# A low half of weights on GpSimd beside the convolution taps, and a seventh up tile by seven block products

## The chip, the cores and the metric

The kernel runs on one core of a Trainium2 chip. The metric is the device time of one execution in microseconds, the median of the runs shown. The engines are called by their short names: PE (TensorE, matrix products, with PEld for its weight loads), DVE (VectorE), ACT (ScalarE), POOL (GpSimd) and SP (the engine that issues most of the weight loads).

## The reference

Two layers on a sequence of 512 rows with 1024 channels, everything in 32-bit floats. Each layer has a mixer, a gated feed-forward network (FFN) with a short causal convolution, and a per-layer embedding. The change lies in the FFN, which each layer runs once:

```python
def conv_ffn(xn, w_up, conv_w, conv_b, w_down):
    S = xn.shape[1]
    h = xn @ w_up                                    # 1024 -> 2 x 2816 channels
    hp = jnp.pad(h, ((0, 0), (CONV_WIDTH - 1, 0), (0, 0)))
    c = conv_b + sum(hp[:, t:t + S] * conv_w[t] for t in range(CONV_WIDTH))
    g, u = jnp.split(c, 2, axis=-1)
    return (jax.nn.silu(g) * u) @ w_down             # 2816 -> 1024

for i in range(DEPTH):                               # DEPTH = 2
    xn = rmsnorm(h, norm_mix[i])
    h = h + (mixer_a(...) if i < 1 else mixer_b(...))
    h = h + conv_ffn(rmsnorm(h, norm_ffn[i]), ...)
    h = h + per_layer_embed(h, p[i], ...)
return rmsnorm(h, norm_final)
```

## The kernel before

**Products in halves.** A weight is cut into a high half `wh`, which ACT rounds (L203), and a low half `wl` = weight minus `wh`, which DVE subtracts (L204). The activations are cut in the same way. A product is three matmuls, high by high, high by low and low by high (`mm3`, L234). The channels lie on the partitions and the 512 rows of the sequence are the columns of the moving matrix.

**The weights' way.** SP fetches the weights piece by piece into staging buffers that take turns under three names (`staged`: `wraw`, and the sums `wsum` below). The halves of at most 1024 columns are called units. There are four buffers each for `wh` and `wl` (`WBUFS`), and `pump` writes the cast and the subtraction of a unit up to four units ahead of the matmuls that use it. A unit's buffer comes free only when PE has done with the unit four before it.

**The up tiles.** Each layer's FFN has 22 tiles of 2 x 128 up channels, here numbered 0 to 21. A plain tile is 48 matmuls of 512 columns (two PSUM banks, `up`, 8 blocks of the input, three products each) and two units of 1024 columns. A woven tile (the numbers in `UPS`) is made by seven products of blocks in Strassen's manner (`woven_up`): 84 matmuls of 256 columns, on sums of the inputs that are made once, and on four units (1024, 1024, 1024 and 512 columns) that come from the raw weights and from sums of them (`weave`, three DVE steps L163 to L165 on 512 to 1024 columns). The seven products end in two PSUM tiles `ux` and `uy`; ACT copies (`head`, `side`, L805), and DVE puts them together in SBUF (`minus`, L812, L813).

**After a tile.** `gated` (L755) applies the convolution: for each of the two halves an ACT pass with scale and bias (L760) gives `c`, and two DVE taps (L762) add the rows shifted by one and by two. They read PSUM where the tile is plain and SBUF where it is woven. Then come Silu on ACT and a product on DVE (L769). A class `Pair` takes two finished tiles and makes the sums that the woven down projection needs (L518 to L535, L312).

**The blocks.** The 22 tiles go in three blocks, 0 to 7, 8 to 15 and 16 to 21. Before the down projection of the first and of the second block, the first tile of the next one is already multiplied (tile 8, tile 16), so that DVE can work on its result beside the projection. The two first down projections are woven (`dx`, `dy`, four column chunks, each added to what DRAM holds), the third is plain (`d`). So from the end of tile 5 the order before is: tile 6 plain, tiles 7 and 8 woven, down projection; in the second block tiles 8, 9, 10, 12, 14 are woven, 11, 13, 15 plain, tile 16 woven ahead of the projection; in the third 17, 18, 20, 21 woven and 19 plain.

**Order.** The code is written out by a scheduler that puts each instruction on its engine's queue in the order that its estimate of readiness gives. `behind(a, b)` holds `a` after `b` on the same engine without a semaphore. An engine does its queue in order: a step that waits holds all behind it.

Of the kernel before, what the change touches and what calls it, by code (L numbers as in the profile page):

```python
# [8 lines left out]
F32 = mybir.dt.float32  # L9
F32R = mybir.dt.float32r  # L10
AF = mybir.ActivationFunctionType
ALU = mybir.AluOpType

P = 128
D = 1024
S = 512
# [3 lines left out]
NJ = FF // P  # L20
PARTS = [(0, 8), (8, 16), (16, 22)]
WOVEN = 2
UPS = (7, 8, 9, 10, 12, 14, 16, 17, 18, 20, 21)
ASIDE = {7: 12, 9: 7, 17: 7, 20: 6}
PAIRS = 4
SLOTS = 9
# [26 lines left out]
def tile_yoco(ctx: ExitStack, tc: tile.TileContext, t, out: bass.AP, out_b: bass.AP):  # L53
    nc = tc.nc

    const = ctx.enter_context(tc.tile_pool(name="const", bufs=1))
# [5 lines left out]
    tp = ctx.enter_context(tc.tile_pool(name="tp", bufs=2))  # L62
# [4 lines left out]
    def psum(name):  # L67
        return mmp.tile([P, S], F32, tag="mm", name=name)
# [35 lines left out]
    def plan_ups(l, j0, j1):  # L104
        for j in range(j0, j1):
            (plan_woven if j in UPS else plan_cols)(t["w_up"][l, j : j + 1], 1, *((0, KD) if j in UPS else (KD,)))

# [29 lines left out]
                      [(ap, f"ah{q}", f"al{q}") for q in free[k0 : k0 + 4]] if c else None)  # L137

    units = [(i, q, lo, n) for i, p in enumerate(pieces) for q, (lo, n) in enumerate(p[2])]
    raws, ready, splits, sums = {}, {}, {}, {}  # L140
    state = {"raw": 0, "unit": 0, "next": 0, "tags": [0, 1, 2], "turn": 2, "pt": 0, "sent": {}}

    def behind(ins, front):

        tc.add_manual_dep(ins.ins, front.ins.name,
                          mybir.DependencyInfo(mybir.DependencyClass.NoSync, mybir.DependencyReason.DATA),
                          reason="order")

    def staged(name):
        tags = state["tags"]  # L150
        r = wp.tile([P, 2 * UNIT], F32, tag=f"r{tags[state['turn'] % len(tags)]}", bufs=1, name=name)
        state["turn"] += 1
        return r
# [25 lines left out]
    def pump(upto):  # L179
        while state["unit"] < min(upto, len(units)):  # L180
            i, q, lo, n = units[state["unit"]]
            load(i + 1)
            u = state["unit"]
            own = pieces[i][3]
            if own:
                pool, *tags = own[q]
                wh, wl = (pool.tile([P, n], F32R, tag=tg, name=f"own{u}_{tg}") for tg in tags)
            else:
                wh = wp.tile([P, UNIT], F32R, tag="wh", bufs=WBUFS, name=f"wh{u}")
                wl = wp.tile([P, UNIT], F32R, tag="wl", bufs=WBUFS, name=f"wl{u}")  # L190
            if i in woven:
                src = weave(i, q)
                hi, low = (x[:, :n].rearrange("p (b k m) -> p b k m", b=src.shape[1], m=P) for x in (wh, wl))
            elif i in paired:
                whole = raws[i][:, : pieces[i][1]].rearrange("p (c k n) -> p k c n", c=2, n=256)
                src = whole[:, lo // S : (lo + n) // S]
                hi, low = (x[:, :n].rearrange("p (k c n) -> p k c n", c=2, n=256) for x in (wh, wl))
            else:
                src, hi, low = raws[i][:, lo : lo + n], wh[:, :n], wl[:, :n]
            if u == 0:  # L200
                cast = nc.vector.tensor_copy(hi, src)
            else:
                cast = nc.scalar.copy(hi, src)  # L203
            state["split"] = splits[u] = cast, nc.vector.tensor_sub(low, src, hi.bitcast(F32))  # L204
            ready[u] = (wh, wl, n)
            state["unit"] += 1

    def take():
        u = state["next"]
        pump(u + 1)  # L210
        state["next"] += 1
        return ready.pop(u)
# [38 lines left out]
    def v(name, i):  # L251
        c = VEC[name] + i
        return vec[:, c : c + 1]
# [27 lines left out]
    ps = psum("idle").rearrange("p (a b) -> p a b", a=4)  # L281
    for i in range(IDLE):
        nc.tensor.matmul(ps, idle, idle.rearrange("p (o t) -> p o t", o=1).to_broadcast([P, 4, P]),
                         start=True, stop=True)
    minus_half = const.tile([P, S // 64], F32, name="minus_half")
    nc.vector.memset(minus_half, -0.5)
    ident = const.tile([P, P], F32, name="ident")
# [177 lines left out]
    box = {}  # L465
# [264 lines left out]
    def ffn(l, norm, nxt):  # L730
# [6 lines left out]
        def up(j, later=False):  # L737
            if j in UPS:
                return woven_up(j, later)
            parts = chunk(256, KD)  # L740
            pss = [psum(f"up{j}_{s}") for s in range(2)]
            if j:
                for s in range(2):
                    mm3(pss[s], parts, xs, s * P)
            else:
                for k, ((wh, wl, off), (xh, xl)) in enumerate(zip(parts, xs)):
                    for x, both in ((xh, (wh, wl)), (xl, (wh,))):
                        for s, ps in enumerate(pss):
                            for w in both:
                                nc.tensor.matmul(ps, w[:, off + s * P : off + (s + 1) * P], x,  # L750
                                                 start=k == 0 and x is xh and w is wh, stop=k == KD - 1 and x is xl)
            return pss if later else gated(j, pss)

        def gated(j, pss, fronts=()):
            cs = []  # L755
            for s, ps in enumerate(pss):
                col = s * NJ + j
                cw = [v("conv_w", (l * 3 + i) * 2 * NJ + col) for i in range(3)]
                c = tp.tile([P, S], F32, tag=f"c{s}", name=f"c{j}_{s}")
                nc.scalar.activation(c, ps, AF.Identity, bias=v("conv_b", l * 2 * NJ + col), scale=cw[2])  # L760
                for tap in (1, 2):
                    ins = nc.vector.scalar_tensor_tensor(c[:, tap:], ps[:, : S - tap], cw[2 - tap], c[:, tap:],  # L762
                                                         op0=ALU.mult, op1=ALU.add)
                    if fronts and tap == 1:
                        behind(ins, splits[fronts[s]][1])
                cs.append(c)
            a = tp.tile([P, S], F32, tag="sg", name=f"a{j}")
            box["silu"] = nc.scalar.activation(a, cs[0], AF.Silu)
            nc.vector.tensor_mul(a, a, cs[1])  # L769
            return a  # L770
# [51 lines left out]
        ins = inputs()  # L822
        ahead = up(0)
        behind(splits[state["next"] + 1][1], norm.low)
        for i, (j0, j1) in enumerate(PARTS):
            if i < WOVEN:
# [10 lines left out]
                pss, res = up(j1, later=True), []  # L837
                u = state["next"]
# [103 lines left out]
    for q, k0, k1 in FIRST:  # L942
# [4 lines left out]
        if k0 == 0:  # L947

            (wh, wl, off), = parts
            for x, w, cs in [(x, w, (c, c + 1)) for c in (0, 2) for x, w in ((0, wh), (0, wl), (1, wh))]:  # L950
                for c in cs:
                    nc.tensor.matmul(vps[q][c], xs[0][x][:, c * P : (c + 1) * P], w[:, off : off + S],
                                     start=x == 0 and w is wh, stop=False)
            continue
        if (q, k1) == (0, KD):
# [7 lines left out]
            cast, low = state["split"]  # L963
# [63 lines left out]
    for c in range(4):  # L1027
# [27 lines left out]
    ps = psum("turned")  # L1055
# [287 lines left out]
    last = len(steps)  # L1343
# [56 lines left out]
    pss = [psum(f"gt{i}_0") for i in range(2)]  # L1400
# [236 lines left out]
```

## Time and profile before

| | us |
|---|---|
| timed runs, median of 3 | 1100.64 (1100.06 to 1100.65) |
| span of the profiled execution | 1098.7 |
| median less span | 1.9 |
| PE busy | 1089.1 |
| DVE busy | 959.0 |
| ACT busy | 661.0 |
| GpSimd busy | 125.0 |

The granted TensorE clock is 0.999 over the span. A timeline's row reads: start (us from the span's start), duration, engine, line, operation, result<-operands, shape, count; what stands in square brackets is the idle time just before it and what ended it. A row of stretches has the length, then for each engine its busy time and the instructions that it began, then the granted clock, the DMA engines' share and GB/s. A row of waits has the engine, what waited, what it waited for, and the sum, count and longest of these waits.

### The profile page before, as it was taken

The numbers are of one execution on the slowest core, as the hardware profiler recorded it, in microseconds if no ns is written. First come the engines' busy times: TensorE is split into PE (matmuls) and PEld (weight loads), VectorE is DVE, ScalarE is ACT, GpSimd is POOL, SyncE is SP. The second block draws the span as 40 slices with busy tenths as digits, with TensorE's granted clock in tenths as the row PEclk, the third lists the DMA queues.
The fourth block names the chain that finished last, engine by engine and source line by source line (L and its number), as shares of the span: only waits on it lengthen the run. The fifth ranks groups of instructions, "written<-read, shape, count | busy, mean of one in ns | idle before, by whom it ended". The sixth has DMA issues, their size and how long they took to land.

```text
span 1098.7 us, 17476 instructions
## 1 busy us (share of the span) xinstructions
PE 1089.1 (99%) x6629; PEld 974.4 (89%) x6629; DVE 959.0 (87%) x1540; ACT 661.0 (60%) x1141; POOL 125.0 (11%) x192
## 2 busy tenths in 40 slices
PE   9999999999999999999999999999999999999997
PEld 7888988899998999988888887888999989999886
DVE  5588889999899989877988997799998999898887
ACT  5735666565676656655656775565655666567544
POOL 2200200000100010021114452000001000100200
PEclk9999999999999999999999999999999999999999
DMA  9621674125633267353234216441255333664534
GB/s 317 113 88 39 178 264 150 43 77 116 155 115 116 79 160 222 120 190 112 67 87 135 78 58 227 176 153 39 77 142 128 115 116 86 156 220 142 203 95 98
DMA packets 47508, 144.24 MB, mean 131 GB/s; under 512 B 13048, under 2 KB 18688, under 8 KB 36928
## 3 DMA queue, kind: packets, MB, share of 16 engines
q1 hardware_dynamic: 40560, 128.77, 35.6%
q0 software_dynamic: 5296, 9.70, 6.7%
q10 hardware_dynamic: 1568, 4.65, 1.1%
q8 instruction: 52, 0.85, 0.3%
q14 instruction: 32, 0.26, 0.1%
HBM read 116.89 MB, written 18.88 MB: 124 GB/s over the span
## 4 chain that ended last, share of the span: by engine, by line
PE 95%; DVE 2%; issue 1%; ACT 1%; DMA 0%; SPq 0%; POOLq 0%; POOL 0%; ACTq 0%
PE up L234 20%; PE ux L234 10%; PE dx L234 10%; PE uy L234 8%; PE dy L234 8%; PE d L234 6%; PE q L234 4%; PE gate L234 4%; PE u L234 4%; PE o L234 4%; PE up L750 2%; PE pv L1326 1%; PE v L244 1%; PE v L245 1%; PE v L246 1%; PE pin L234 1%
## 5 line engine op out<-in xcount | busy, mean ns | idle before, releaser
L204 DVE TENSOR_TENSOR wl<-wraw,wh 128x1024 fp32r<-128x1024 f32 (+2 forms) x198 | 217.3, 1102 | 42.8 <-ACT wh L203 41.9
L203 ACT CAST wh<-wraw 128x1024 fp32r<-128x1024 f32 (+2 forms) x197 | 182.8, 933 | 107.6 <-PE up L234 21.8
L203 ACT CAST wh<-wsum 128x1024 fp32r<-128x1024 f32 x84 | 88.3, 1052 | 62.7 <-issue 14.9
L204 DVE TENSOR_TENSOR wl<-wsum,wh 128x1024 fp32r<-128x1024 f32 x84 | 102.5, 1225 | 16.1 <-ACT wh L203 16.0
L762 DVE SCALAR_TENSOR_TENSOR c<-up,vec,c 128x511 f32<-128x511 f32 (+1 forms) x88 | 65.0, 744 | 2.4 <-ACT c L760 1.9
L234 PE MATMUL up<-nf10h,wh 128*128 128x512 f32 x160 | 62.3, 389 | 0.0
L234 PE MATMUL up<-nf00h,wh 128*128 128x512 f32 x160 | 62.3, 389 | 0.0
L234 PE MATMUL up<-nf10l,wh 128*128 128x512 f32 x160 | 62.3, 389 | 0.0
L234 PE MATMUL up<-nf00l,wh 128*128 128x512 f32 x160 | 62.3, 389 | 0.0
L234 PE MATMUL up<-nf00h,wl 128*128 128x512 f32 x160 | 62.1, 389 | 0.0
L234 PE MATMUL up<-nf10h,wl 128*128 128x512 f32 x160 | 62.0, 389 | 0.0
L600 POOL DMA_DIRECT2D saved<-head x16 | 13.9, 871 | 412.9 <-DVE head L720 412.9
L760 ACT ACTIVATE c<-up,vec 128x512 f32<-128x512 f32 x44 | 34.0, 777 | 31.8 <-PE up L234 26.6
L163 DVE TENSOR_TENSOR wsum<-wraw 128x1024 f32<-128x1024 f32 x42 | 51.2, 1220 | 0.6
L234 PE MATMUL ux<-t,wh 128*128 128x256 f32 x264 | 50.4, 283 | 0.0
L234 PEld LDWEIGHTS ux<-t,wh 128*128 128x128 f32 x264 | 41.2, 192 | 0.0
L234 PE MATMUL ux<-t,wl 128*128 128x256 f32 x132 | 37.4, 283 | 0.0
L234 PEld LDWEIGHTS up<-nf00h,wl 128*128 128x128 f32 x160 | 30.0, 188 | 6.2
L234 PEld LDWEIGHTS up<-nf10h,wl 128*128 128x128 f32 x160 | 30.0, 188 | 6.2
L234 PEld LDWEIGHTS up<-nf00l,wh 128*128 128x128 f32 x160 | 30.0, 188 | 6.2
L234 PEld LDWEIGHTS up<-nf10l,wh 128*128 128x128 f32 x160 | 30.0, 188 | 6.2
L234 PEld LDWEIGHTS up<-nf10h,wh 128*128 128x128 f32 x160 | 30.0, 188 | 6.0
(769 smaller groups left out, 3734.3 us busy)
## 6 DMA issues: line engine op xcount, KB each, us to landing
wraw<-in_w_up SPq DMA_DIRECT2D x44, 1024.0 KB, 5.6
wraw<-in_w_down SPq DMA_DIRECT2D x16, 1024.0 KB, 5.0
wraw<-in_w_gate SPq DMA_DIRECT2D x8, 1024.0 KB, 5.5
wraw<-in_w_down SPq DMA_DIRECT2D x8, 768.0 KB, 4.5
wraw<-in_w_u SPq DMA_DIRECT2D x4, 1024.0 KB, 9.4
wraw<-in_w_out SPq DMA_DIRECT2D x4, 1024.0 KB, 4.9
saved<-head POOLq DMA_DIRECT2D x16, 256.0 KB, 4.2
saved<-tail POOLq DMA_DIRECT2D x16, 256.0 KB, 4.1
```

The lines of the kernel that those rows point to most:

```text
L163: nc.vector.tensor_add(s[:, 0::3], g[:, 1:2].to_broadcast([P, 2, k, P]), g[:, 0::3])
L203: cast = nc.scalar.copy(hi, src)
L204: state["split"] = splits[u] = cast, nc.vector.tensor_sub(low, src, hi.bitcast(F32))
L234: return [nc.tensor.matmul(ps, w, x, start=first and j == 0, stop=last and j == len(todo) - 1, skip_group_check=onto) for j, (w, x) in enu ...
L244: nc.tensor.matmul(ps, xh[:, s], wh[:, a:b], start=st, stop=False)
L245: nc.tensor.matmul(ps, xl[:, s], wh[:, a:b], start=False, stop=False)
L246: nc.tensor.matmul(ps, xh[:, s], wl[:, a:b], start=False, stop=en)
L600: box["onto"] = nc.gpsimd.dma_start(x, y, accum_op=ALU.add)
L750: nc.tensor.matmul(ps, w[:, off + s * P : off + (s + 1) * P], x, start=k == 0 and x is xh and w is wh, stop=k == KD - 1 and x is xl)
L760: nc.scalar.activation(c, ps, AF.Identity, bias=v("conv_b", l * 2 * NJ + col), scale=cw[2])
L762: ins = nc.vector.scalar_tensor_tensor(c[:, tap:], ps[:, : S - tap], cw[2 - tap], c[:, tap:], op0=ALU.mult, op1=ALU.add)
L1326: nc.tensor.matmul(ps, lhs, rhs, start=j == 0, stop=j == len(todo) - 1)
```

## The change

Three things change.

- Tile 6 becomes woven (`UPS` gains 6). So tiles 6, 7 and 8 are woven in a row, ahead of the first down projection, in each layer.
- In each tile that stays plain (0 to 5, 11, 13, 15, 19) the order of the gating changes: both ACT passes come first, then a DVE copy of one column of the second one's result, called `sign`, then the four taps in the order first half, second half, first, second. All four are held behind the copy.
- One unit that stands two ahead of the next one to be taken at that moment gets its low half from GpSimd instead of DVE, and GpSimd starts it when the copy `sign` is done (`after`, with a semaphore). There are 20 such units.

The instructions of PE grow by 72 matmuls (2 x 36), those of DVE and ACT by 14 each, those of GpSimd by 20.

```diff
-UPS = (7, 8, 9, 10, 12, 14, 16, 17, 18, 20, 21)
+UPS = (6, 7, 8, 9, 10, 12, 14, 16, 17, 18, 20, 21)
...
+    def after(ins, front):
+
+        tc.add_manual_dep(ins.ins, front.ins.name,
+                          mybir.DependencyInfo(mybir.DependencyClass.Sync, mybir.DependencyReason.DATA),
+                          reason="start")
...
-            state["split"] = splits[u] = cast, nc.vector.tensor_sub(low, src, hi.bitcast(F32))
+            start = shadows.pop(u, None)
+            lows = (nc.gpsimd if start else nc.vector).tensor_sub(low, src, hi.bitcast(F32))
+            if start:
+                after(lows, start)
+            state["split"] = splits[u] = cast, lows
...
+    sign = const.tile([P, 1], F32, name="sign")
...
-            return pss if later else gated(j, pss)
+            return pss if later else gated(j, pss, shadow=True)
...
+            if shadow:
+                taps = []
+                for s, ps in enumerate(pss):
+                    col = s * NJ + j
+                    c = tp.tile([P, S], F32, tag=f"c{s}", name=f"c{j}_{s}")
+                    nc.scalar.activation(c, ps, AF.Identity, bias=v("conv_b", l * 2 * NJ + col),
+                                         scale=v("conv_w", (l * 3 + 2) * 2 * NJ + col))
+                    taps += [(c, ps, tap, v("conv_w", (l * 3 + 2 - tap) * 2 * NJ + col)) for tap in (1, 2)]
+                    cs.append(c)
+                with tc.high_priority():
+                    last = nc.vector.tensor_copy(sign, cs[1][:, :1])
+                    shadows[state["next"] + 2] = last
+                    for c, ps, tap, w in taps[::2] + taps[1::2]:
+                        ins = nc.vector.scalar_tensor_tensor(c[:, tap:], ps[:, : S - tap], w, c[:, tap:],
+                                                             op0=ALU.mult, op1=ALU.add)
+                        behind(ins, last)
+                        last = ins
+                a = tp.tile([P, S], F32, tag="sg", name=f"a{j}")
+                box["silu"] = nc.scalar.activation(a, cs[0], AF.Silu)
+                nc.vector.tensor_mul(a, a, cs[1])
+                return a
```

**Where it moves instructions.** The first place is DVE's row at the end of tile 5 in layer 0, before. `c5_0` and `c5_1` are tile 5's two halves, `wl51` is the first low half of tile 7 (tile 6 is still plain here, and its two units are older), `a5` is the gated tile, and `t03` an input sum.

```order
L762 SCALAR_TENSOR_TENSOR c5_0_2199<-up5_0_2149,vec_84,c5_0_2199 128x510
L204 TENSOR_TENSOR wl51_2228<-wraw26_2225,wh51_2227 128x1024
L312 TENSOR_TENSOR t03_2134<-x0_1sq_2126,t02_2133 128x512
L204 TENSOR_TENSOR wl52_2236<-wsum26_2229,wh52_2235 128x1024
L762 SCALAR_TENSOR_TENSOR c5_1_2203<-up5_1_2150,vec_84,c5_1_2203 128x511
L762 SCALAR_TENSOR_TENSOR c5_1_2203<-up5_1_2150,vec_84,c5_1_2203 128x510
L769 TENSOR_TENSOR a5_2207<-a5_2207,c5_1_2203 128x512
```

After, at the same place (`wl52` is the last unit of tile 6, `wl53` the first of tile 7; GpSimd's one here is `wl51`, tile 6's third unit):

```order
L323 TENSOR_TENSOR t03_2140<-x0_1sq_2132,t02_2139 128x512
L777 COPY sign_132<-c5_1_2211 128x1
L780 SCALAR_TENSOR_TENSOR c5_0_2209<-up5_0_2159,vec_84,c5_0_2209 128x511
L780 SCALAR_TENSOR_TENSOR c5_1_2211<-up5_1_2160,vec_84,c5_1_2211 128x511
L780 SCALAR_TENSOR_TENSOR c5_0_2209<-up5_0_2159,vec_84,c5_0_2209 128x510
L780 SCALAR_TENSOR_TENSOR c5_1_2211<-up5_1_2160,vec_84,c5_1_2211 128x510
L211 TENSOR_TENSOR wl52_2246<-wraw25_2145,wh52_2245 128x512
L786 TENSOR_TENSOR a5_2218<-a5_2218,c5_1_2211 128x512
L169 TENSOR_TENSOR wsum26_2278<-wraw26_2274 128x2x512
```

Tile 7's first low half stood ahead of tile 5's last taps; now it stands behind the marker, the four taps, tile 5's product and tile 7's weave sums. How far behind, the next rows of the same engine show (after, ten rows on):

```order
L171 TENSOR_TENSOR wsum26_2278<-wsum26_2278,wraw26_2274 128x512
L211 TENSOR_TENSOR wl53_2277<-wraw26_2274,wh53_2276 128x1024
L211 TENSOR_TENSOR wl54_2311<-wsum26_2278,wh54_2310 128x1024
L211 TENSOR_TENSOR wl55_2340<-wsum26_2278,wh55_2339 128x1024
L844 TENSOR_TENSOR line6_2239<-line6_2239,side6_2240 128x256
L845 TENSOR_TENSOR gate6_2238<-gate6_2238,uy6_2237 128x512
```

Three low halves of tile 7 stand ahead of the sums that end tile 6. On PE the turn from tile 6 to tile 7 reads, after (`ux`, `uy` are the woven tile's two PSUM tiles; `t0_rh`, `t0_rl` and `nf00h0` and the like are halves of the inputs and of their sums):

```order
L244 MATMUL ux6_2236<-t0_rh_1947,wl52_2246 128x256
L244 MATMUL ux7_2373<-nf00h0_987,wh53_2276 128x256
L244 MATMUL ux7_2373<-nf00l0_988,wh53_2276 128x256
L244 MATMUL uy7_2374<-nf00h1_989,wh53_2276 128x256
L244 MATMUL uy7_2374<-nf00l1_990,wh53_2276 128x256
L244 MATMUL ux7_2373<-nf00h0_987,wl53_2277 128x256
```

Four matmuls with the high half are drawn ahead of the first one that needs the low half. The second place is ACT's row at the end of tile 7, after (`wh62` is the cast of a sum `wsum28`, which DVE makes):

```order
L322 CAST act0_3_0_2501<-a7_2498 128x512
L209 CAST wh62_2584<-wsum28_2552 128x1024
L322 CAST act0_3_1_2502<-act0_3t_2370 128x512
L837 COPY side8_2518<-uy8_2515 128x256
L322 CAST act0_3_2_2503<-act0_3u_2504 128x512
```

The copy `side8`, for which PE waits in tile 8 before it writes `uy8` again, stands on ACT behind the cast `act0_3_1`, whose operand `act0_3t` DVE makes.

More of the change, by code (lines that the diff above doesn't have):

```diff
@@ L139, in tile_yoco @@
     units = [(i, q, lo, n) for i, p in enumerate(pieces) for q, (lo, n) in enumerate(p[2])]
-    raws, ready, splits, sums = {}, {}, {}, {}
+    raws, ready, splits, sums, shadows = {}, {}, {}, {}, {}
     state = {"raw": 0, "unit": 0, "next": 0, "tags": [0, 1, 2], "turn": 2, "pt": 0, "sent": {}}
@@ L751, in up, with gated @@
                                                  start=k == 0 and x is xh and w is wh, stop=k == KD - 1 and x is xl)
-            return pss if later else gated(j, pss)
-        def gated(j, pss, fronts=()):
+            return pss if later else gated(j, pss, shadow=True)
+        def gated(j, pss, fronts=(), shadow=False):
             cs = []
+            if shadow:
[19 more added lines that the diff above has]
+                return a
             for s, ps in enumerate(pss):
```

## Prediction

> **What bounds the kernel now.** I read the page first, then the waits, the stretches tile by tile, and last the rows of TensorE (PE) and VectorE (DVE) at the places where the order changes.
>
> ```profile
> span 1098.7 us, 17476 instructions
> PE 1089.1 (99%) x6629; PEld 974.4 (89%) x6629; DVE 959.0 (87%) x1540; ACT 661.0 (60%) x1141; POOL 125.0 (11%) x192
> PE 95%; DVE 2%; issue 1%; ACT 1%; DMA 0%; SPq 0%; POOLq 0%; POOL 0%; ACTq 0%
> ```
>
> PE is busy all the time and the chain that ended last is PE's. So a matmul taken away is worth its own time, and a wait put on PE is lost in full.
>
> ```profile
> PE idle L283 <- DVE minus_half L286: 1.1, 1, 1.1
> PE v L952 <- ACT n00h L307: 0.4, 1, 0.4
> PE uy L234 <- ACT side L805: 0.3, 2, 0.2
> ```
>
> These are the longest waits of PE. The third is small, but it lies where the change works: at the end of tile 8, once in each layer. (Tiles count from 0: the seventh is tile 6.)
>
> ```profile
> 208.00:219.00 11.00, 11.00 (x50) 9.12 (x49) 10.83 (x18) 6.29 (x10) 0.00 (x0) 1.00 0.29 98
> 219.00:229.70 10.70, 10.70 (x49) 8.84 (x48) 8.77 (x13) 5.04 (x8) 0.00 (x0) 1.00 0.00 0
> 229.70:239.80 10.10, 10.10 (x85) 10.04 (x84) 9.17 (x14) 6.96 (x12) 0.00 (x0) 1.00 0.29 105
> 239.80:250.80 11.00, 10.85 (x91) 10.64 (x90) 11.00 (x17) 8.50 (x15) 0.00 (x0) 1.00 0.27 95
> ```
>
> These are tiles 5, 6, 7 and 8 of layer 0 (after the length: PE, its loads, DVE, ACT, GpSimd). In tile 8 DVE is full, 11.00 of 11.00. The low halves show what this means:
>
> ```profile
> 217.14 1.22 DVE L204 TENSOR_TENSOR wl<-wraw,wh 128x1024 fp32r<-128x1024 f32 x1
> 229.68 0.28 PE L234 MATMUL ux<-nf00h,wh 128*128 128x256 f32 x1
> 242.03 1.40 DVE L762 SCALAR_TENSOR_TENSOR c<-out,vec,c 128x510 f32<-128x510 f32 x2
> 243.35 1.22 DVE L163 TENSOR_TENSOR wsum<-wraw 128x1024 f32<-128x1024 f32 x1
> 244.48 0.74 DVE L762 SCALAR_TENSOR_TENSOR c<-out,vec,c 128x510 f32<-128x510 f32 x1
> 245.15 0.68 DVE L164 TENSOR_TENSOR wsum<-wsum,wraw 128x512 f32<-128x512 f32 x1
> 245.75 0.69 DVE L769 TENSOR_TENSOR a<-a,c 128x512 f32<-128x512 f32 x1
> 246.95 0.42 DVE L532 TENSOR_TENSOR act_3t<-a,a 128x256 f32<-128x256 f32 x1
> 247.29 0.41 DVE L533 SCALAR_TENSOR_TENSOR act_3u<-act_3t,a 128x256 f32<-128x256 f32 x1
> 249.17 1.21 DVE L204 TENSOR_TENSOR wl<-wraw,wh 128x1024 fp32r<-128x1024 f32 x1
> 250.78 0.28 PE L234 MATMUL dx<-edge,wl 128*128 128x256 f32 x1
> ```
>
> Tile 7's first low half is ready at 218.36, 11.3 us before the tile starts at 229.68. Two block-product tiles later, that of the down projection is ready at 250.38 and used at 250.78: 0.4 us is left. Two such tiles in a row eat nearly all of DVE's lead. The change puts a third ahead of them.
>
> The starts of neighbouring rows give what a step takes of DVE when it is full: 1.13 us for 1024 columns, 0.60 for 512, 0.34 for 256, 0.66 for a tap.
>
> **The change, part by part.**
>
> (a) PE. Tile 6 loses 48 matmuls of 512 columns and gets 84 of 256.
>
> ```profile
> 435.17 10.91 PE up L234 x48
> 397.40 2.88 PE dx L234 x24
> ```
>
> 48 take 10.9 us, 84 at 0.120 us take 10.1 us: 0.8 us less, in two layers -1.7 us if nothing waits.
>
> (b) GpSimd takes one low half of 1024 columns beside each plain tile, 20 in all, and DVE gets 20 copies of one column (a step of 256 columns takes 0.34 us, above; these take less, and I count nothing).
>
> ```profile
> 598.72 0.87 POOL L1341 TENSOR_TENSOR ol<-side,oh 128x128 fp32r<-128x128 f32 x2
> 537.90 1.29 POOL L342 TENSOR_TENSOR n1acc<-n1acc,n1sq 128x512 f32<-128x512 f32 x1 [3.84 <-ACT n1sq L337]
> 537.93 0.68 DVE L920 TENSOR_TENSOR z<-gate,np0rstd 128x512 f32<-128x512 f32 x1
> 1042.06 1.28 POOL L342 TENSOR_TENSOR np1acc<-np1acc,np1sq 128x512 f32<-128x512 f32 x1 [4.06 <-ACT np1sq L337]
> 1042.10 2.33 DVE L204 TENSOR_TENSOR wl<-wraw,wh 128x1024 fp32r<-128x1024 f32 x1
> ```
>
> 128 columns take 0.44 us, 512 take 1.29, so 1024 are estimated at 2.4 us. Beside GpSimd a DVE step that reads PSUM keeps its 0.68 us, but one with two SBUF operands waits it out (2.33 instead of 1.22). The four taps read PSUM and last 4 x 0.66 = 2.64 us, so GpSimd's 2.4 us are covered. Where GpSimd's half belongs to the next tile's third unit (tiles 12, 14, 16, 20) it is needed 5.8 us after the plain tile's end and ready after 3.9. I take nothing; the other end is in the second rival.
>
> (c) The marker copy waits for the second ACT pass of the plain tile, and all four taps stand behind it. Before, the first two taps were done while PE was still in the tile. DVE so idles at the end of each plain tile and has 1.3 us more to do behind it. That costs nothing in tiles 0 to 4, where low halves are over 9 us early, but counts behind tiles 5 and 15.
>
> ```profile
> 218.77 1.05 ACT L203 CAST wh<-wsum 128x1024 fp32r<-128x1024 f32 x1 [0.61 <-PE up L234]
> 218.80 0.39 PE L234 MATMUL up<-nf00h,wh 128*128 128x512 f32 x1
> 219.73 0.77 ACT L760 ACTIVATE c<-up,vec 128x512 f32<-128x512 f32 x1
> ```
>
> Tile 5 ends at 218.80. ACT has a cast ahead of the pass, now of 512 columns (0.5 us), so the pass ends 1.3 us after the tile, and the taps start at 1.4.
>
> (d) DVE from there. A woven tile adds the three weave sums, its low halves (3.5 units for 2), and two sums at its end. Its four units also hold all four weight buffers, so tile 7's units are only cast as tile 6 frees them. In the new order, from the taps to tile 7's first low half: 4 taps 2.64, 2 steps of 1024 2.26, 7 of 512 4.20, 3 of 256 1.02: 10.1 us, so it is ready 11.6 us after tile 5's end. PE gets there after 10.1 + 0.5 (four high-half matmuls drawn ahead): it waits 1.1 us.
> From there to the first low half of the down projection: 8 of 1024 9.04, 13 of 512 7.80, 7 of 256 2.38, 8 taps 5.28: 24.5 us, and 0.4 us for a cast that waits for tile 7's last copy. That gives 11.6 + 24.5 + 0.4 = 36.5 us after tile 5's end. PE alone needs 3 x 10.1 + 0.5 = 30.7. So PE waits 5.8 us in all, most of it at tile 8's end: there the copy `side8` stands on ACT behind a cast that needs DVE's late product, and then the low half itself is late.
> Before, the same place came 250.78 - 218.80 = 32.0 us after tile 5's end. Net +4.5 us.
>
> (e) Second block: tile 15 is plain, 16 woven, then the down projection. From the marker to its first low half stand the same 10.1 us of DVE work, so 11.6 us after tile 15's end. Before:
>
> ```profile
> 364.10 0.28 PE L234 MATMUL ux<-nf00h,wh 128*128 128x256 f32 x1
> 374.77 0.28 PE L234 MATMUL dx<-edge,wl 128*128 128x256 f32 x1
> 766.62 0.39 PE L234 MATMUL up<-nf10h,wh 128*128 128x512 f32 x1
> 798.60 0.28 PE L234 MATMUL dx<-edge,wl 128*128 128x256 f32 x1
> ```
>
> 10.7 us; net +1.0 us. In the third block (19, 20, 21) the low half that is needed 10.3 us after tile 19 comes at about 8.7. Layer 1 goes through the same: 798.60 - 766.62 is again 32.0.
>
> (f) One more woven tile shifts the turn of the three staging buffers, so the last piece of `w_o` goes out behind two other pieces.
>
> ```profile
> wraw<-in_w_up SPq DMA_DIRECT2D x44, 1024.0 KB, 5.6
> ```
>
> A piece lands about 5.6 us after its issue. Pieces are cast several units ahead of PE, so I take nothing; the other end is one landing in full, +5.6 us once.
>
> Sum: 2 x (4.5 + 1.0) = +11.0 us (the -1.7 of PE is in it). The profiled span of 1098.7 becomes 1109.7. The timed runs lie 1.9 us above that span (median 1100.64): 1111.6 us.
>
> Bounds: the wait cannot go below nothing (-1.7 us). If each step took its full row length and not the start-to-start time (1.22, 0.69, 0.42, 0.74: a tenth more), DVE would be 3.5 us later per layer in the first block and 1 in the second: +20 us. I stay at the start-to-start times, since DVE's queue is full there, as in the rows of 242 to 250.
>
> **The rivals.**
>
> First, faster: DVE's lateness stays hidden and PE's own time decides, 1100.64 - 1.7 = 1098.9 us. For it: PE hardly waits today, DVE's mean is 87%, and GpSimd relieves it by 20 x 1.13 us. Against: the relief falls in plain tiles, where DVE had 10 us of lead and cannot use more, since the buffers are full. It decides if DVE's 34.6 us of work from tile 5 to the down projection took under 28.9, a sixth less than the rows say.
>
> Second, GpSimd collides with DVE. If its half ran 3.4 us or started late, the low half behind the taps would wait for it, up to 0.8 us, at the four places that count: +3, 1115 us.
>
> Third, the clock. The gap before `uy` in tile 8 would be 3.4 us, the longest inside the kernel.
>
> ```profile
> 1.13 3.69 PE L283 MATMUL idle<-idle 128*128 128x512 f32 x9 [1.13 <-DVE minus_half L286]
> 1091.13 0.28 PE L246 MATMUL gt<-own_al,np10h 128*128 128x256 f32 x1
> 1094.00:1096.00 2.00, 0.00 (x0) 0.00 (x0) 0.55 (x1) 0.61 (x1) 0.11 (x1) 1.00 0.23 90
> 1096.00:1098.60 2.60, 0.00 (x0) 0.00 (x0) 0.00 (x0) 0.00 (x0) 0.00 (x0) 0.56 0.36 133
> ```
>
> The nine first matmuls take 0.41 us each, against 0.227 in the plain tiles: a cold start costs 1.6 us. At the end the granted clock was still 1.00 up to 1096, 4.6 us after the last matmul. A gap of 3.4 us would thus not lower it; if it did, +3.2 us, 1115 us. The Trainium skill, "TensorE: Matmul & The Clock Gate", section "Why this matters for your kernels", says that gaps of more than about 3 us between matmul bursts bring the clock back to half. By that rule the sum would be 1115; this trace, with 4.6 us at full clock, does not bear it out.
>
> Fourth, the copies on ACT overlap better than I count, and only half of the lateness reaches PE: +5, 1106 us.
>
> **How the numbers follow.** Forecast (1108 to 1114) 0.58; collision or clock (to 1118) 0.17; half of it (1104.5 to 1108) 0.10; no change that can be told 0.06; faster 0.09. A measurement of this kernel tells about 0.2%, 2.2 us, from no change. So slower 0.85, same 0.06, faster 0.09. The range 1104.5 to 1118 takes in the first three.
>
> **What would show it.** PE's longest waits: `uy` for ACT's `side` and `dx` for DVE's `wl`, 3 to 5 us together, once per layer; `ux` for `wl` at tile 7 about 1 us; `dx` for `wl` in the second block about 1 us. Tile 6's start to the first `dx` with `wl` 36.5 instead of 32.0. GpSimd's `wl` about 2.4 us, DVE's taps unchanged at 0.74. I am wrong if PE still runs through tiles 6 to 8 without waits (then DVE's order or its times are not what I summed), or if the loss lies outside the two FFNs.

## The result, and the profile after

The changed kernel takes 1113.82 us (median of 4 runs, 1112.57 to 1116.58) against 1100.57 us (4 runs, 1100.06 to 1100.65): ratio 1.0123, 95% interval 1.0111 to 1.0135. It is slower by 13.3 us. The profiled execution has a span of 1112.0 us. The page's head and its chain:

```profile
span 1112.0 us, 17668 instructions
PE 1090.6 (98%) x6701; PEld 977.6 (88%) x6701; DVE 944.7 (85%) x1554; ACT 666.9 (60%) x1155; POOL 173.9 (16%) x212
PE 84%; DVE 8%; issue 2%; ACT 2%; DMA 2%; SPq 1%; POOL 0%; POOLq 0%; DVEq 0%; ACTq 0%
```

DVE is busy for 14 us less than before, and the time is 13 us longer: DVE now has 8% of the chain (2% before). A mean says nothing of the place. PE's longest waits name it (the first wait of the kernel, 1.1 us as before, is left out):

```profile
PE uy L244 <- ACT side L837: 5.4, 2, 2.7
PE dx L244 <- DVE wl L211: 3.3, 4, 0.9
PE ux L244 <- DVE wl L211: 1.9, 2, 1.0
PE ux L244 <- ACT line L567: 0.7, 2, 0.4
PE gt L256 <- DVE wl L211: 0.5, 1, 0.5
```

Layer 0 in the timeline, PE's rows at tile 6's start, tile 7's first low half, tile 8's end, the projection's first low half, and the same in the second block:

```profile
219.38 0.28 PE L244 MATMUL ux<-nf00h,wh 128*128 128x256 f32 x1
231.03 0.38 PE L244 MATMUL ux<-nf00h,wl 128*128 128x256 f32 x1 [0.97 <-DVE wl L211]
253.57 0.39 PE L244 MATMUL uy<-nf00h,wh 128*128 128x256 f32 x1 [2.72 <-ACT side L837]
255.96 0.39 PE L244 MATMUL dx<-edge,wl 128*128 128x256 f32 x1 [0.70 <-DVE wl L211]
380.87 0.38 PE L244 MATMUL dx<-edge,wl 128*128 128x256 f32 x1 [0.95 <-DVE wl L211]
```

What stands behind these waits is DVE's row from tile 5's end, and the end of the chain there, which is DVE's until PE takes it over:

```profile
218.38 0.69 DVE L323 TENSOR_TENSOR t<-x_1sq,t 128x512 fp32r<-128x512 f32 x1 [0.76 <-ACT t L322]
220.68 0.15 DVE L777 COPY sign<-c 128x1 f32<-128x1 f32 x1 [1.62 <-ACT c L772]
220.75 2.71 DVE L780 SCALAR_TENSOR_TENSOR c<-up,vec,c 128x511 f32<-128x511 f32 x4
223.38 0.68 DVE L211 TENSOR_TENSOR wl<-wraw,wh 128x512 fp32r<-128x512 f32 x1
...
229.75 1.22 DVE L211 TENSOR_TENSOR wl<-wraw,wh 128x1024 fp32r<-128x1024 f32 x1
```

```profile
253.49 0.63 DVE act L323 x2
254.12 0.57 issue
254.69 1.23 DVE wl L211
255.96 1.45 PE dx L244 x10
```

To tell the runs apart, the span is cut at PE's rows: tile 0's first matmul, the last matmul of each down projection, and the end. A block thus reaches to the end of its projection; two numbers are layers 0 and 1; "rest" is all that lies outside the blocks.

| us | block 1 | block 2 | block 3 | rest | span |
|---|---|---|---|---|---|
| before | 137.0, 137.1 | 124.0, 124.0 | 84.1, 84.1 | 408.5 | 1098.7 |
| after | 141.8, 141.7 | 124.9, 124.9 | 84.3, 84.3 | 410.0 | 1112.0 |
| difference | +4.7, +4.7 | +0.9, +0.9 | +0.3, +0.3 | +1.6 | +13.3 |

### The profile page after: what moved, and what is told of

Read it like the earlier page. It is cut to its first block, busy times and chain, and to the rows that moved or that the text cites. A ratio compares the mean times of both kernels' runs of the same rounds, so it can differ in the third digit from the quotient of the medians.

```text
span 1112.0 us, 17668 instructions
## 1 busy us (share of the span) xinstructions
PE 1090.6 (98%) x6701; PEld 977.6 (88%) x6701; DVE 944.7 (85%) x1554; ACT 666.9 (60%) x1155; POOL 173.9 (16%) x212
## 4 chain that ended last, share of the span: by engine, by line
PE 84%; DVE 8%; issue 2%; ACT 2%; DMA 2%; SPq 1%; POOL 0%; POOLq 0%; DVEq 0%; ACTq 0%
PE up L244 18%; PE dx L244 10%; PE ux L244 9%; PE uy L244 7%; PE dy L244 7%; PE q L244 4%; PE gate L244 4%; PE u L244 4%; PE o L244 4%; PE d L244 3%; PE up L761 2%; DVE wl L211 2%; PE pv L1358 1%; PE v L254 1%; PE v L255 1%
## 5 line engine op out<-in xcount | busy, mean ns | idle before, releaser
L209 ACT CAST wh<-wraw 128x512 fp32r<-128x512 f32 (+2 forms) x197 | 181.7, 928 | 120.6 <-PE uy L244 18.0
L211 DVE TENSOR_TENSOR wl<-wraw,wh 128x1024 fp32r<-128x1024 f32 (+2 forms) x188 | 204.3, 1091 | 36.4 <-ACT wh L209 35.7
L211 DVE TENSOR_TENSOR wl<-wsum,wh 128x1024 fp32r<-128x1024 f32 x78 | 95.1, 1226 | 11.4 <-ACT wh L209 11.4
L211 POOL TENSOR_TENSOR wl<-wsum,wh 128x1024 fp32r<-128x1024 f32 x10 | 24.1, 2413 | 213.4 <-PE ux L244 213.4
L244 PE MATMUL up<-nf10h,wh 128*128 128x512 f32 x144 | 56.1, 390 | 0.0
L244 PE MATMUL up<-nf00h,wl 128*128 128x512 f32 x144 | 55.9, 389 | 0.0
L244 PE MATMUL up<-nf10h,wl 128*128 128x512 f32 x144 | 55.7, 389 | 0.0
L780 DVE SCALAR_TENSOR_TENSOR c<-up,vec,c 128x511 f32<-128x511 f32 (+1 forms) x80 | 54.2, 741 | 0.0
L211 POOL TENSOR_TENSOR wl<-wraw,wh 128x1024 fp32r<-128x1024 f32 x10 | 24.1, 2406 | 102.7 <-DVE sign L777 86.0
L1302 ACT ACTIVATE prs<-prs,neg 128x129 f32<-128x129 f32 x64 | 25.3, 397 | 13.3 <-DVE neg L1297 12.5
```

The lines of the kernel that those rows point to most:

```text
L211: lows = (nc.gpsimd if start else nc.vector).tensor_sub(low, src, hi.bitcast(F32))
L244: return [nc.tensor.matmul(ps, w, x, start=first and j == 0, stop=last and j == len(todo) - 1, skip_group_check=onto) for j, (w, x) in enu ...
L1302: ins = nc.scalar.activation(pr[:, e, :], pr[:, e, :], AF.Exp, bias=neg[:, e : e + 1], scale=-1.0, accum_out=sm[:, e : e + 1])
```

## The experiments

Each was timed against the kernel before on the same chip; times below are medians, ratios stand with their 95% interval. Below, "marker" stands for the copy `sign`, the new order of the four taps, their hold behind the copy and the high priority that the diff gives them all; no run takes the priority alone. The first theory was the prediction's: three woven tiles in a row use up DVE's lead, and the marker adds to it.

**Only the woven tile.**

```diff
-UPS = (7, 8, 9, 10, 12, 14, 16, 17, 18, 20, 21)
+UPS = (6, 7, 8, 9, 10, 12, 14, 16, 17, 18, 20, 21)
```

> Only the seventh woven tile: UPS gains 6, the gating and all low halves stay as before. Theory (DVE has too little lead for three woven tiles in a row, and the marker adds to it): without the marker DVE starts 1.3 us earlier behind tile 5 and has two taps less to do there (1.3 us), but makes one low half more (1.13 us): 1.5 us less late per layer in the first block, and no wait at all in the second (1.1 us per layer in the changed kernel). So about 1113.8 - 2 x (1.5 + 1.0) = 1109 us. Rival (the marker with its taps makes the loss, the woven tile would fit): 1098.9 us.

Measured: 1101.77 us, ratio 1.0011 (1.0002 to 1.0020). Neither number came: the theory was 7 us too high. Block 1 is 137.8 in both layers, +0.7. PE's waits:

```profile
PE uy L234 <- ACT side L805: 0.7, 2, 0.3
PE dx L234 <- ACT wh L203: 0.5, 2, 0.2
```

DVE is full here too, but its order is another:

```profile
225.77 1.22 DVE L204 TENSOR_TENSOR wl<-wraw,wh 128x1024 fp32r<-128x1024 f32 x1
242.52 1.85 DVE L204 TENSOR_TENSOR wl<-wraw,wh 128x512 fp32r<-128x512 f32 x2
244.28 0.75 DVE L762 SCALAR_TENSOR_TENSOR c<-out,vec,c 128x511 f32<-128x511 f32 x1
```

Tile 7's first low half starts at 225.77 (229.75 after the change; 0.8 of these 4.0 us is the later start of the whole layer), and the second of the two at 242.52 is the projection's first one, ahead of tile 7's taps; after the change it stands at 254.69, behind the sums of the last pair. PE is given projection matmuls while tile 8 waits, and the chain at tile 8's end is mostly PE's:

```profile
246.54 0.47 PE dx L234 x4
247.02 1.68 PE ux L234 x12
248.69 0.95 PE dx L234 x8
```

**Only the GpSimd halves, with marker and moved taps** (`UPS` as before).

> Only GpSimd's low halves with the marker and the moved taps; UPS as before. Theory: behind tile 6 DVE starts 1.3 us later and has two taps more (1.3 us), less one low half (1.13), and 0.4 us of lead: about 1.1 us of wait before the first down projection per layer; in the second block the same 1.0 us as in the changed kernel. So 1100.6 + 2 x 2.1 = 1105 us. Rival that the marker makes the whole loss: about 1115 us. Rival that the shadow is free and only the woven tile costs: 1100.6 us, with no wait in the second block.

Measured: 1107.8 us, ratio 1.0070 (1.0057 to 1.0084). Block 1 +1.8 per layer, block 2 +0.9 and +1.2, block 3 +0.3. More than half of the loss comes without the woven tile, against what I expected. The theory's places hold, its sum was 3 us short.

```profile
PE dx L244 <- DVE wl L211: 3.9, 4, 1.0
PE uy L244 <- ACT side L837: 1.4, 3, 0.6
```

The two halves of the change make +1.4 and +7.4 us alone, and together +13.3: they do not add up.

**The woven tile in the third block**, tile 19 in place of tile 6, no marker.

```diff
-UPS = (7, 8, 9, 10, 12, 14, 16, 17, 18, 20, 21)
+UPS = (7, 8, 9, 10, 12, 14, 16, 17, 18, 19, 20, 21)
```

> The kernel before with tile 19 woven in place of tile 6 (so again one woven tile more per layer, but in the third block, where no sums of pairs are made); no marker, no GpSimd halves. Theory: low halves there are 3.6 to 9 us early and stay level from woven tile to woven tile (3.7 us ahead at tile 17, 3.9 at tile 18), so PE's own saving is all that is left: 1100.6 - 1.7 = 1098.9 us, no new waits. Rival (a third and fourth woven tile in a row costs DVE's lead anywhere, 5.5 us per tile as in the first block): waits of 2 us or more before tile 21 or the plain down projection, 1104 us or more.

Measured: 1105.01 us, ratio 1.0040 (1.0026 to 1.0054). The theory fell: block 3 is 1.1 and 1.6 us longer, though PE saves 0.84 there. The longest waits are behind the last tile, not at low halves:

```profile
PE d L234 <- ACT act21h L311: 1.4, 2, 0.7
PE gt L246 <- DVE wl L204: 0.5, 1, 0.5
```

I had read only how early the low halves were. The last tile's own result, which the projection needs at once, came late. In layer 0 that is about half of the loss of 2.0 us (1.1 and the 0.84 not saved); by the starts of PE's rows the rest is four delays of 0.2 to 0.4 us in the tiles ahead of it, most of which a list of waits does not show.

**The low halves first in DVE's order.**

```diff
+SOON = (53, 61, 103, 192, 200, 242)
...
+            if u in SOON:
+                with tc.high_priority():
+                    lows = nc.vector.tensor_sub(low, src, hi.bitcast(F32))
```

> The changed kernel, with high priority for three low halves per layer: the first one of tile 7, and the first ones of the two woven down projections, so that DVE makes them ahead of the sums of pairs (edit moves the order of DVE and ACT, no work). Theory (DVE's throughput): the waits at tile 7's start and in the second block go (1.1 us each per layer), but in the first block DVE is full from tile 5 to the projection, so the lateness shows up behind, at the copy `side` or at the next low halves: about 2 us per layer less at best in the sum of both blocks, 1110 us (1109 to 1112). Rival (only the order of DVE's queue is at fault): all new waits go, about 1100 us.

Measured: 1108.97 us, ratio 1.0077 (1.0064 to 1.0089), near the theory's 1110 and just below its range. Block 2's wait is gone (124.0). Block 1 is still 141.2 and 139.8: the wait has moved to a low half of the tiles.

```profile
PE ux L249 <- DVE wl L216: 3.5, 2, 1.7
PE uy L249 <- ACT side L842: 0.7, 2, 0.3
```

Layer 0 is 1.4 us longer than layer 1 because the granted clock fell behind that wait. The stretches around it, with the clock as third column from the end:

```profile
239.00:241.90 2.90, 1.16 (x10) 0.95 (x9) 2.90 (x6) 2.71 (x5) 0.00 (x0) 1.00 0.00 0
243.30:246.40 3.10, 3.10 (x17) 3.10 (x16) 2.35 (x4) 1.28 (x2) 0.00 (x0) 0.50 0.40 90
246.40:248.00 1.60, 1.60 (x15) 1.60 (x15) 1.43 (x2) 1.60 (x4) 0.00 (x0) 0.99 0.98 415
```

For 3.1 us PE began 17 matmuls where about 26 fit at 0.120 us. So the order alone is not at fault, and a wait can cost more than its length. The next runs ask which of the markers costs, and what in it.

**No marker in tiles 5 and 15, and its complement.**

```diff
-            return pss if later else gated(j, pss, shadow=True)
+            return pss if later else gated(j, pss, shadow=j not in (5, 15))
```

> The changed kernel, but tiles 5 and 15 keep the old gating (no marker, no GpSimd half); the markers stay in the other eight plain tiles. In this order DVE's row behind tile 5 is that of the woven-only kernel, with the projection's first low half ahead of tile 7's taps. Theory (the loss is made by the marker at the two plain tiles that stand last before woven ones and a projection): first block +0.7 us per layer as in the woven-only kernel, second block nothing, third block 0.3 (marker of tile 19): 1100.5 + 2 x 1.0 and some tenths for the start = 1103 us. Rival (every marker costs its share): a fifth of the markers gone, about 1111 us.

Measured: 1104.9 us, ratio 1.0034 (1.0022 to 1.0047); block 1 138.4 and 138.3, block 2 124.2 and 123.8.

```diff
+            return pss if later else gated(j, pss, shadow=j in (5, 15))
```

> The complement: marker, held taps and GpSimd half only in tiles 5 and 15 of each layer, tile 6 woven, all other plain tiles as before. Theory: nearly the whole loss remains, first block +4.7 us and second block +0.9 per layer: 1100.5 + 2 x 5.6 = 1112 us. Rival (every marker costs its share): a fifth of the markers, on top of the woven-only kernel, about 1104 us.

Measured: 1114.55 us, ratio 1.0125 (1.0111 to 1.0138); block 1 141.7 and 142.5, block 2 125.1. On top of the woven tile, the four markers in tiles 5 and 15 of the two layers make most of the loss; the other sixteen cost about 3 us together (1104.9 against 1101.8). The waits are those of the changed kernel:

```profile
PE uy L244 <- ACT side L837: 5.4, 2, 2.7
PE dx L244 <- DVE wl L211: 2.6, 3, 0.9
```

**GpSimd's halves without marker and hold.** The gating is the old one; GpSimd starts behind the first tap.

```diff
+                    if shadow and s == 0 and tap == 1:
+                        shadows[state["next"] + 2] = ins
```

> The changed kernel with GpSimd's 20 low halves, but without the marker and the hold: the taps stand in the old order, and GpSimd starts behind the first tap of the plain tile. Theory (the late start and the two taps moved behind the tile's end make the loss, GpSimd's work does not): no wait in the second block, the first as in the woven-only kernel; GpSimd and DVE steps with two SBUF operands may now run at the same time and wait for each other, up to 1.1 us per tile, against 1.13 us that DVE is relieved of: 1102 us (1100 to 1105). Rival (GpSimd's low half itself, late or in DVE's way, makes the loss): 1110 us or more.

Measured: 1104.9 us, ratio 1.0035 (1.0022 to 1.0049): block 1 138.1 and 138.3, block 2 124.6. With twenty GpSimd halves and no marker, 9 us of the 13 are gone.

**The marker without GpSimd.** The twenty low halves stay on DVE.

```diff
-            lows = (nc.gpsimd if start else nc.vector).tensor_sub(low, src, hi.bitcast(F32))
+            lows = nc.vector.tensor_sub(low, src, hi.bitcast(F32))
```

> The changed kernel with marker and held taps, but the 20 low halves stay on DVE. The order of DVE has the projection's first low half ahead of tile 7's taps, as in the woven-only kernel. Theory (DVE's time behind the marker is what is short, in whatever order): 1.13 us more per layer than in the kernel with the lows put first in the first block (there +4.2 and +2.7), and 1.1 us more in the second than the changed kernel: 1116 us (1112 to 1119). Rival (only the place of the projection's low half in DVE's order matters): first block as woven-only, 1103 us. Rival (GpSimd was the cause): 1102 us, with no wait in the second block.

Measured: 1115.7 us, ratio 1.0135 (1.0121 to 1.0149): block 1 141.1 and 141.0, block 2 125.9. GpSimd's work is a help where the marker stands, not the cause: without it block 2 is 1.0 us longer than in the changed kernel, and block 3 0.9 and 0.7 us. Block 1 is 0.7 us shorter, for its order is another. Here the projection's low half is early in DVE's order, and PE waits for the low halves of the tiles instead:

```profile
PE ux L244 <- DVE wl L211: 5.7, 4, 1.5
PE dx L244 <- DVE wl L211: 3.0, 2, 1.5
```

**The marker on the first half.** It copies from `cs[0]`, and the taps stand in the old order behind it.

```diff
-                    last = nc.vector.tensor_copy(sign, cs[1][:, :1])
+                    last = nc.vector.tensor_copy(sign, cs[0][:, :1])
...
-                    for c, ps, tap, w in taps[::2] + taps[1::2]:
+                    for c, ps, tap, w in taps:
```

> The changed kernel with the marker taken from the first half's ACT pass in place of the second's, and the taps in the old order (first half's two, then the second half's two), still held in a row behind it; GpSimd's 20 halves stay. The first half's taps can then run while PE is still in the tile. Theory (waiting for the second pass, 1.3 us, and two taps moved behind the tile's end, 1.3 us, make the loss): nearly all of it goes; GpSimd now runs beside DVE steps with two SBUF operands, as in the kernel without the hold: first block +1.1 us per layer, second +0.6: 1104.5 us (1102 to 1106). Rival (any marker and hold costs, wherever it stands): 1112 us or more.

Measured: 1115.45 us, ratio 1.0135 (1.0121 to 1.0149); block 1 142.2 and 143.4, block 2 125.8. The theory's number fell, but the run does not tell what the late start alone costs, for something else came with it. The early start let GpSimd run beside a DVE step that reads SBUF twice:

```profile
219.48 0.74 DVE L780 SCALAR_TENSOR_TENSOR c<-up,vec,c 128x510 f32<-128x510 f32 x1
220.14 2.74 DVE L323 TENSOR_TENSOR t<-x_1sq,t 128x512 fp32r<-128x512 f32 x1
```

```profile
219.93 2.40 POOL L211 TENSOR_TENSOR wl<-wsum,wh 128x1024 fp32r<-128x1024 f32 x1 [9.00 <-ACT wh L209]
```

The tap (PSUM) keeps its 0.74 us; the step `t` takes 2.74 instead of 0.69 and ends 0.55 us after GpSimd. This is the collision of the prediction's second rival, 2.05 us at once where that allowed 0.8, and tile 6 waits for `t` and then, through ACT, for `side`, and the clock falls behind that wait, in both layers:

```profile
229.58 0.39 PE L244 MATMUL uy<-nf00h,wh 128*128 128x256 f32 x1 [2.08 <-ACT side L837]
```

```profile
230.20:233.20 3.00, 3.00 (x16) 3.00 (x16) 2.62 (x4) 1.17 (x2) 0.00 (x0) 0.50 0.00 0
786.50:789.50 3.00, 3.00 (x16) 3.00 (x15) 2.97 (x4) 1.04 (x1) 0.00 (x0) 0.50 0.03 5
```

The Trainium skill, "SBUF — State Buffer", section "SBUF: two separate sides", says that a GpSimd step and a DVE step with two SBUF inputs exclude each other for a whole instruction, whichever starts first. The two rows agree: the DVE step seems to start at 220.14, but ends 0.55 us behind GpSimd's end at 222.33.

**One DVE step more, no marker.** In the woven-only kernel, tile 7's first weave sum is made twice.

```diff
+            if i in (26, 77):
+                nc.vector.tensor_add(s[:, 0::3], g[:, 1:2].to_broadcast([P, 2, k, P]), g[:, 0::3])
             nc.vector.tensor_add(s[:, 2], s[:, 3], g[:, 0])
```

> The woven-only kernel with one DVE step of 1024 columns more per layer (the first weave sum of tile 7 is made twice; result unchanged). The longer work also moves the projection's first low half behind the sums of the last pair in DVE's order, where the changed kernel has it, while there is no marker. Theory (DVE's time is short there): 1.1 us more per layer, up to 1.5 with the switches of PE: 1101.8 + 2.3 = 1104 us (1103 to 1105). Rival (the place of that low half in DVE's order makes the loss of the changed kernel): first block +4 us or more per layer, 1108 us or more. Rival (DVE has room behind tile 5 when there is no marker): 1101.8 us.

Measured: 1110.96 us, ratio 1.0097 (1.0083 to 1.0111). The rival on the order was right in its number: 1.1 us of DVE work per layer cost 4.3 and 4.6 us in block 1 (142.1, 142.4). By the table below the order is only a part of it: in layer 0 1.7 us are DVE's later sum, 2.6 the longer rest of the block. The scheduler had put the projection's first low half behind the pair's sums, PE had nothing else to do at tile 8's end, and the clock fell after the wait:

```profile
PE uy L236 <- ACT side L807: 6.4, 4, 2.7
```

```profile
250.80:253.60 2.80, 0.08 (x2) 0.08 (x1) 2.66 (x7) 2.76 (x6) 0.00 (x0) 1.00 0.00 0
254.70:257.90 3.20, 2.93 (x14) 2.64 (x13) 3.20 (x4) 0.85 (x2) 0.00 (x0) 0.50 0.00 0
```

**What joins these runs.** In block 1, the sum that ends tile 8 on DVE (`gate`, L845 of the changed kernel) was timed from tile 0's first matmul, and the rest of the block from there. In the changed kernel that matmul starts at 154.06, and the sum's row is:

```profile
258.43 0.68 DVE L845 TENSOR_TENSOR gate<-gate,uy 128x512 f32<-128x512 f32 x1
```

| layer 0, us | DVE's sum ends at | the block ends later by | low half of the projection |
|---|---|---|---|
| before | 100.7 | 36.3 | late |
| woven tile only | 102.8 | 35.0 | early |
| taps not held | 103.1 | 35.0 | early |
| no marker in 5, 15 | 103.4 | 35.0 | early |
| lows on DVE | 106.1 | 35.0 | early |
| lows first | 106.3 | 35.0 | early |
| marker on the first half | 107.3 | 35.0 | early |
| woven, ACT first (below) | 103.0 | 34.5 | early |
| changed kernel | 105.1 | 36.7 | late |
| marker in 5, 15 only | 105.0 | 36.7 | late |
| shadow only | 102.2 | 36.7 | late |
| tile 5 woven (below) | 101.4 | 36.7 | late |
| one step more | 104.4 | 37.6 | late |

"Early" is ahead of tile 7's taps, "late" behind the sums of the last pair. Over 4.5 us of lateness the rest of the block is the same 35.0 us in six kernels, and the waits and clock drops ahead of that point are in the first number. What makes the second number is how far PE had come when the sum started: of the projection's 336 matmuls it had begun 39 in these six kernels, 24 or 25 in the four of 36.7, 28 before, 44 and 17 in the other two. At 0.12 us for each (24 take 2.88 us, as the prediction shows), these counts give the differences to within 0.15 us. So a late low half costs 1.7 us on top, because PE gets to fewer projection matmuls beside tile 8; the 17 of "one step more" hold about 1 us of clock loss. That DVE's row sets the end is read from its nearly full queue up to that sum and from PE's waits; no run makes DVE faster and leaves all else. For the changed kernel's block 1 this gives +0.7 for the woven tile (PE's 0.84 saved in it), +2.3 for the marker (105.1 against 102.8, with GpSimd's help in it), +1.7 for the order: 4.7. It is a division by two runs, not three single causes, for the late order came with the marker in some kernels and without it in others (one step more, tile 5 woven). Why the scheduler turns it round was not followed.

**Two tries at a better version.** Tile 5 woven in place of 6:

```diff
+UPS = (5, 7, 8, 9, 10, 12, 14, 16, 17, 18, 20, 21)
...
-                        for q in ((2,), (3, 0), (1,), ())[p]:
+                        for q in ((2, 3), (0, 1), (), ())[p]:
```

> A version that might beat both: tile 5 woven in place of tile 6, so that plain tile 6 lies between it and tiles 7 and 8; the input sums are made one pair earlier; no marker, no GpSimd halves. Theory: DVE regains some 2 us in the plain tile, so it reaches the projection late by at most 1.5 us per layer; with PE's 0.84 us per layer saved: 1100.8 us (1099 to 1103). Rival (any seventh woven tile in the first block costs what it does in place 6): 1101.8 us.

Measured: 1103.9 us, ratio 1.0035 (1.0022 to 1.0047), above the theory's range. DVE's sum came earlier (101.4 in layer 0), but the projection's low half was late in the order, 36.7 again, and PE waited for it:

```profile
PE dx L234 <- DVE wl L204: 2.8, 2, 1.9
```

The woven-only kernel with ACT's copy and the pair's casts first:

```diff
-            nc.scalar.copy(side, other[:, second])
+            with tc.high_priority():
+                nc.scalar.copy(side, other[:, second])
...
+            with tc.high_priority():
+                for src, (hi, lo) in ((b, self.own), (t, self.ones), (u, self.twos)):
+                    split(src, hi, lo)
```

> The woven-only kernel with high priority for the casts and subtractions that end a pair and for the copy `side`, so that on ACT the copy stands ahead of two of the casts at tile 8's end (order moved, no work). Theory (what is left of the loss there, about 0.7 us net per layer, is PE waiting for ACT's copy and a cast, both late behind DVE): the copy's wait of 0.3 us per layer goes, the rest stays: 1101.2 us (1100.3 to 1102). Rival (ACT's order makes all that is left): PE's saving appears, 1099 us.

Measured: 1101.44 us, ratio 1.0009 (1.0000 to 1.0018), as the theory said. The wait for `side` is gone, one for a low half has come (`dy` for `wl`, 0.5 us per layer). No version beat the kernel before.

## Why the prediction was right, and what in it was wrong

The sum was +11.0 us and the measured one +13.3.

- (a) Tile 6 takes 10.1 us instead of 10.9, as said.
- (b) GpSimd's half was put at 2.4 us. Its row, and the taps beside it (0.74 before):

```profile
L211 POOL TENSOR_TENSOR wl<-wsum,wh 128x1024 fp32r<-128x1024 f32 x10 | 24.1, 2413 | 213.4 <-PE ux L244 213.4
L780 DVE SCALAR_TENSOR_TENSOR c<-up,vec,c 128x511 f32<-128x511 f32 (+1 forms) x80 | 54.2, 741 | 0.0
```

- (c) The taps were to start 1.4 us after tile 5's end; they start at 220.75, 1.37 after 219.38.
- (d) Tile 7's first low half was to be ready after 11.6 us: 229.75 + 1.22 - 219.38 = 11.6. PE's first use of the projection's low half was to come after 36.5: 255.96 - 219.38 = 36.6, net +4.6 where +4.5 stood. The gap before `uy` was 2.72 us where 3.4 stood, and 0.36 us of waiting for ACT's `line` had come ahead of it.
- (e) Second block: +1.0 predicted, 0.95 of wait in its row.
- (f) No wait of PE for `w_o` came; nothing was right.
- Not in the sum: third block +0.3 per layer (put at nothing), 0.6 ahead of tile 0, 1.1 from the last projection to the end, of which a wait of `gt` for a low half is 0.5. Together, less 0.15 between the layers, these are 2.1 of the missing 2.3 us; the rest lies in the first two blocks, 11.2 where 11.0 stood. The stretch ahead of layer 0's tile 0, which the change does not touch, varied from 153.3 to 154.6 us over the fourteen kernels, and the one behind the last projection by 1.8 us; their causes stay open, as does that of `gt`'s wait.

**The step that failed is the reason given ahead of the sum.** "Two such tiles in a row eat nearly all of DVE's lead. The change puts a third ahead of them" points at the woven tile. Alone it costs 1.4 us. Without it 7.4 us of loss remain, without the markers in tiles 5 and 15 4.1 us: neither alone makes the 13.3, and the markers are the larger part. The sum came out because it was added up along the changed kernel's own order, in which marker, taps and late low half all stand. Asked what one half of the change would do, the same reasoning missed by 7 us, since that kernel has an order of its own, which I had not read before I wrote the expectation.

Of the rivals: the first (PE's saving decides) did not come, not even with the woven tile alone. The second (collision) did not happen in the changed kernel, where taps cover GpSimd, but with the marker on the first half it did, at 2.05 us where 0.8 was allowed. The third, the clock, did not decide in the profiled execution of the changed kernel: behind 2.72 us of waiting the clock stayed at full, in both layers.

```profile
250.80:253.50 2.70, 0.06 (x1) 0.00 (x0) 2.70 (x7) 2.61 (x6) 0.00 (x0) 1.00 0.00 0
253.50:256.00 2.50, 1.72 (x13) 1.52 (x13) 2.50 (x4) 2.11 (x4) 0.00 (x0) 1.00 0.00 0
```

But I had dropped that rival too lightly, since four other kernels show it (below). The fourth, half of the lateness hidden on ACT, did not come: block 1 is 4.7 us longer in both layers.

## What to carry to other kernels

A marker that holds an engine until another has finished moves work from under a tile to behind it; that costs little where there is lead (here about 3 us for sixteen markers), and much where the engine has none (9 us for four). Look where the lead ends, and not at the engine's mean. When work is added to or taken from an engine that a scheduler orders, read the new order of each variant before its time is forecast: here 1.1 us of work turned two steps round and cost 4.3 us, about 1 of it through the clock.

## What was not expected of the hardware

The clock. Waits of PE of 1.74 us (the lows first, layer 0), 2.08 us (the marker on the first half, both layers) and 2.72 us (one step more, both layers, and the marker in 5 and 15 only, one layer) were followed by some 3 us at a granted clock of 0.50:

```profile
808.40:811.40 3.00, 2.94 (x14) 2.65 (x14) 3.00 (x4) 0.98 (x2) 0.00 (x0) 0.50 0.00 0
```

That is layer 1 of the last one; in its layer 0, and in the changed kernel, a wait of the same length at the same place was followed by the full clock, and so was the wait of 1.74 us in layer 1 with the lows first. A drop costs 0.8 to 1.4 us: so much longer is the layer with the drop than the other one in the marker in 5 and 15 only and in the lows first. From the end of the kernel before, where the clock stayed full for 4.6 us, I had concluded that such gaps do nothing; one place cannot tell that. The Trainium skill, "TensorE: Matmul & The Clock Gate", section "Part 1: The HAM clock gate (the "warmup" mystery)", says that the clock is set by PE's activity in a window of about 3.4 us that runs freely, so that the same gap can fall into it in one way or another. Low stretches of some 3 us, and drops in one layer but not in the other, agree with that. But the wait of 1.74 us that was enough here is shorter than the page's idle window, and than the 3 us that the prediction quoted; the measurement decides. The timed runs of the changed kernel spread over 4 us (1112.57 to 1116.58), those of the kernel before over 0.6. Their mean clocks do not sort them: 0.996 in the longest, 0.997 in the shortest, 0.999 in the two between. Whether such drops make that spread was not shown.
